# A decoder trunk on one core: down products in the seven-product form, chained sums in PSUM, weight sums on GpSimd

## The chip, the cores and the metric

The kernel runs on one core of a Trainium2 chip. TensorE (PE in the profile, PEld for its weight loads), VectorE (DVE), ScalarE (ACT), GpSimd (POOL) and SyncE (SP, which issues the loads here) run side by side, each with its own queue in order. The metric is the time of one execution on the device, in microseconds.

## The reference, cut to what matters

Two layers work on 512 tokens of 1024 features (all float32): a feed-forward half, a mixer (gated convolution and forgetting attention), cross-attention over 256 memory tokens, and a second feed-forward half; so there are four feed-forward halves. The change touches these alone:

```python
def swiglu(h, w_gu, w_down):
    gate, up = jnp.split(h @ w_gu, 2, axis=-1)        # w_gu: 1024 x 5632
    return (jax.nn.silu(gate) * up) @ w_down          # w_down: 2816 x 1024
x = x + 0.5 * swiglu(rmsnorm(x, g_ffn1[l]), w_ffn1_gu[l], w_ffn1_down[l])
```

## The kernel before, in words

**Precision.** Each operand of a product is split into two float32r parts: hi is a cast on ScalarE, lo = source - hi a subtraction on VectorE (`split`, L197; for weights L157 and L158 in `Weights.prefetch`). `mm3` (L192, its matmul is L195) makes one product as three matmuls: hi.hi, hi.lo, lo.hi.

**Layout.** x stands with its features on the partitions, as eight tiles of 128 x 512 tokens. The 2816 hidden columns are cut into six chunks (`CHUNKS`): chunk 0 has 256, the others 512 each.

**Gate and up products.** Chunk 0 is computed plainly. For each other chunk, gates and ups are the two column halves of one product; with tokens and input features halved too, seven products of quarter size (Winograd's form, numbers 1 to 7) take the place of eight. They need sums of activations (`FfnNormed.prepare`, L465, once per half) and of weight blocks (`Weights.quads`, L68): four sums (t1 to t4) for each of two row halves, on VectorE (L76). A product (`product`, L500) has two units of weights, 128 x 1024 each, and 24 matmuls that move 512 columns: weights are the moving side, activations the stationary one. It uses two PSUM banks of its own (out of eight), for two token tiles. Reads after a product: 1 and 7 are copied by ScalarE (L517); 2, 6, 5, 4 and 3 are read by VectorE, which adds earlier results: fourteen additions of 128 x 512 a chunk. SiLU is on ScalarE, the product with the ups on VectorE (L454).

**Down products.** When a chunk is done, `turn` (L563) transposes it on TensorE (16 transposes through an identity matrix, L569) and splits the rows into hi and lo. `down` (L572) then makes two output tiles at a time; weights are stationary and the 512 tokens move. VectorE adds half the result to x (L579). `ffn_plan` (L1154) writes the order out by hand: a chunk's four downs stand among the seven products of the next chunk, in the order 1, turn, 7, down, 2, down, 6, down, 5, 4, 3, down. At the end of a half the last downs hand each new tile of x at once to `after.add`, the work for the next stage's norm. In the last half, `leave` (L587) makes the last chunk's downs with tokens on the partitions.

**Weights.** All weight blocks are listed in the order of their use. `load` fills a pool of 12 buffers of 128 x 1024 (`big`), issued on SyncE as blocks are let go; `prefetch` splits a unit two units ahead of its use (`AHEAD`), into a pool of three hi and three lo buffers, and makes a block's sum just before its split.

Of the kernel before, what the change touches and what calls it, by code (L numbers as in the profile page):

```python
# [24 lines left out]
CHUNKS = (256, 512, 512, 512, 512, 512)  # L25

# [7 lines left out]
T_BUFS = 56  # L34


class Weights:
    """The weights in the order of their use: loaded ahead, split into two float32r parts."""

    def __init__(self, nc, big_pool, unit_pool):  # L40
        self.nc, self.big_pool, self.unit_pool = nc, big_pool, unit_pool
        self.raws, self.units, self.limits = [], [], []
        self.loaded = self.freed = self.split = self.taken = 0
        self.tiles, self.ready = {}, {}
        self.limit, self.slow = 0, 0
# [22 lines left out]
    def quads(self, w, c0, n):  # L68
        """The seven products' blocks for n columns of the gates and of the ups."""
        r, tmp = {}, {}  # L70

        def raw(q, h):
            r[q, h] = self.raw(w, 2 * h + (4 if q[0] == "2" else 0), 2, (c0 + (DFF if q[1] == "2" else 0), n))

        def tt(out, a, b, op):
            self.nc.vector.tensor_tensor(out=out, in0=a, in1=b, op=op)  # L76
# [8 lines left out]
        def t3(h):  # L85
            tmp[h] = self.big((P, 2, n))
# [14 lines left out]
        def product(i):  # L101
            for h in range(2):
# [69 lines left out]
def trunk(ctx, tc, a, consts, out):  # L172
# [4 lines left out]
    tpool = ctx.enter_context(tc.tile_pool(name="t", bufs=T_BUFS))  # L177
    spool = ctx.enter_context(tc.tile_pool(name="small", bufs=8))
# [13 lines left out]
    def mm3(ps, lhs, rhs, first, last):  # L192
        pairs = ((lhs[0], rhs[0]), (lhs[0], rhs[1]), (lhs[1], rhs[0]))
        for i, (x, y) in enumerate(pairs):
            mm(ps, x, y, start=first and i == 0, stop=last and i == 2)  # L195
# [60 lines left out]
    for l in range(DEPTH):  # L256
        for which in (1, 2):
# [22 lines left out]
            for op, c, i in ffn_plan():  # L280
                c0 = sum(CHUNKS[:c])
                if op == "plain":
                    W.block(gu, 2 * i, 2, (c0, 256), (DFF + c0, 256))
                elif op == "product":
                    if c not in product:
                        product[c] = W.quads(gu, c0, CHUNKS[c])
                    product[c](i)
                elif op == "down" and l == DEPTH - 1 and which == 2 and c == len(CHUNKS) - 1:
                    W.limit = 4
                    W.unit(W.raw(dn, c0 // P + 2 * (i % 2), 2, (512 * (i // 2), 512)), keep=True)  # L290
                elif op == "down":
                    W.block(dn, c0 // P, CHUNKS[c] // P, (256 * i, 256))
# [36 lines left out]
    class Scale:  # L329
        """x is held with its tokens scaled, to be of like size wherever tokens are added: times d."""  # L330
# [9 lines left out]
        def change(self, norm):  # L340
            """Every token to a root mean square of one."""
# [7 lines left out]
    def rsqrt_mean(out, v, width, eps=None):  # L349
        """out = (v / width + eps) ** -0.5"""  # L350
# [52 lines left out]
    class Normed:  # L403
        """x times a gain, in two parts; its 1/rms is applied to what comes of it."""
# [20 lines left out]
    class FfnNormed:  # L425
        """x times a gain as the left sides of the seven products: tokens and features in halves."""
# [15 lines left out]
        def column(self):  # L442
            """1/rms for the gates, and at the scale of x for the ups."""
# [14 lines left out]
        def part(self, i, k):  # L458
            """The two parts of row tile k of product i's left side."""
# [32 lines left out]
    def swiglu_half(n, after=None, early=None):  # L492
        """x += 1/2 * SwiGLU; `after` takes the new tiles of x.

        Gates and ups are the two halves of one product's columns; with halves of the tokens and of
        the features, seven products of quarters (Winograd's form) make the four results.
        """
        s, act, turned, banks = {}, {}, {}, []

        def product(c, i):  # L500
            m = CHUNKS[c]
            bank = [PS()[:, :m] for _ in range(2)]
            for h in range(2):
                w = W.take()
                for k in range(2):
                    for e in range(2):
                        mm3(
                            bank[e], [z[:, e * P : (e + 1) * P] for z in n.part(i, 2 * h + k)],
                            [z[:, k, :] for z in w], h == k == 0, h == k == 1,
# [3 lines left out]
            for e in range(2):  # L513
                ps = bank[e]
                if i in (1, 7):
                    s[i, e] = T()[:, :m]
                    nc.scalar.copy(out=s[i, e], in_=ps)  # L517
                elif i == 2:
                    act[c, e] = g = T()[:, :m]
                    nc.vector.tensor_add(out=g, in0=ps, in1=s[1, e])  # L520
                    n.silu(g, g, e)
                elif i == 6:
                    v = s[1, e]
                    nc.vector.tensor_add(out=v, in0=ps, in1=v)
                    nc.vector.tensor_add(out=s[7, e], in0=v, in1=s[7, e])
                elif i == 5:
                    s[5, e] = T()[:, :m]
                    nc.vector.tensor_add(out=s[5, e], in0=ps, in1=s[7, e])
                    nc.vector.tensor_add(out=s[1, e], in0=ps, in1=s[1, e])
                elif i == 4:  # L530
                    act[c, 2 + e] = g = s.pop((7, e))
                    nc.vector.tensor_add(out=g, in0=ps, in1=g)
                    n.silu(g, g, 2 + e)
                    n.times(g, s.pop((5, e)), 2 + e)
# [679 lines left out]
```

## Time and profile before

| | us |
|---|---|
| median of 3 runs | 2163.15 (2163.04 to 2163.84) |
| span of the profiled execution | 2162.5 |
| PE busy | 2134.3 |
| PEld busy | 1782.3 |
| DVE busy | 1631.1 |
| ACT busy | 1033.1 |
| POOL busy | 95.6 |

The profile is of one execution, whose own time is its span. An engine is busy while at least one of its instructions runs; matmuls overlap each other, so durations of single matmuls don't add up, and the distance from start to start is what one costs. The granted clock of TensorE is 0.999 of full speed in the mean. A row of a group gives its line (of a helper, where a helper issues it), its engine, the operation, written and read tiles, shapes and count.

### The profile page before, as it was taken

To read this page: it belongs to the slowest core of one execution; us is meant where nothing else is said; L and a number is where in the kernel's file an instruction comes from. 1 tells how busy PE (TensorE), PEld (TensorE's weight loads), DVE (VectorE), ACT (ScalarE), POOL (GpSimd) and SP (SyncE) were. 2 spreads that over 40 slices of the span, in tenths; PEclk is the share of its full clock that TensorE was granted. 3 is DMA by queue.
4 is the path that set the end of the run, shared out by engine and by line. 5 is a ranking of instruction groups with operands and counts; after the bars stand their busy time and mean duration, and the time that the engine had idled before them with its cause. 6 is when DMAs were issued, how large, how long until landed. Compare 5 with 4: busy or idle time off the path is not lost.

```text
span 2162.5 us, 26168 instructions
## 1 busy us (share of the span) xinstructions
PE 2134.3 (99%) x10082; PEld 1782.3 (82%) x10082; DVE 1631.1 (75%) x2249; ACT 1033.1 (48%) x1544; POOL 95.6 (4%) x107
## 2 busy tenths in 40 slices
PE   7999999999999999999999999999999999999998
PEld 6888888788888888888888888878888888888887
DVE  6987777668755688888798887767786547987785
ACT  6433434566544554444454443346664445534343
POOL 0000000023001000000000000001220010000000
PEclk9999999999999999999999999999999999999999
DMA  5333332123552133323413333402243521333321
GB/s 179 120 106 111 117 97 69 49 78 92 152 146 88 59 108 107 97 91 101 131 58 117 95 111 98 140 27 69 80 129 114 137 75 53 117 107 117 107 78 40
DMA packets 218371, 214.56 MB, mean 99 GB/s; under 512 B 9230, under 2 KB 167174, under 8 KB 218246
## 3 DMA queue, kind: packets, MB, share of 16 engines
q1 hardware_dynamic: 218214, 212.88, 32.2%
q8 instruction: 79, 1.29, 0.3%
q14 instruction: 46, 0.38, 0.1%
q10 hardware_dynamic: 32, 0.01, 0.0%
HBM read 210.77 MB, written 2.10 MB: 98 GB/s over the span
## 4 chain that ended last, share of the span: by engine, by line
PE 92%; DVE 4%; ACT 3%; issue 1%; DMA 0%; POOL 0%; SPq 0%; DVEq 0%; POOLq 0%; ACTq 0%
PE ps L195 88%; PE ps L569 2%; ACT whi L157 1%; DVE wlo L158 1%; DVE t L835 1%; ACT t L813 1%; PE ps L807 0%; PE ps L844 0%; DVE t L376 0%; PE ps L1040 0%; PE ps L828 0%; DVE t L852 0%; DMA big<-in_x 0%; ACT big L794 0%; DVE t L675 0%
## 5 line engine op out<-in xcount | busy, mean ns | idle before, releaser
L157 ACT CAST whi<-big 128x1024 fp32r<-128x1024 f32 x516 | 536.7, 1040 | 885.3 <-PE ps L195 673.4
L195 PE MATMUL ps<-t,whi 128*128 128x512 f32 x2784 | 861.7, 390 | 1.7 <-ACT whi L747 1.4
L195 PE MATMUL ps<-whi,t 128*128 128x512 f32 x2624 | 830.7, 391 | 1.8 <-ACT t L199 1.8
L158 DVE TENSOR_TENSOR wlo<-big,whi 128x1024 fp32r<-128x1024 f32 x516 | 622.5, 1209 | 193.9 <-ACT whi L157 191.8
L195 PEld LDWEIGHTS ps<-t,whi 128*128 128x128 f32 x2784 | 520.6, 188 | 109.6 <-ACT whi L747 1.9
L195 PEld LDWEIGHTS ps<-whi,t 128*128 128x128 f32 x2624 | 493.8, 188 | 105.1 <-ACT t L199 2.5
L195 PE MATMUL ps<-t,wlo 128*128 128x512 f32 x1392 | 542.2, 389 | 1.1 <-DVE wlo L748 1.1
L195 PE MATMUL ps<-wlo,t 128*128 128x512 f32 x1312 | 511.6, 390 | 0.0
L195 PEld LDWEIGHTS ps<-t,wlo 128*128 128x128 f32 x1392 | 261.2, 188 | 56.1 <-DVE wlo L748 1.9
L195 PEld LDWEIGHTS ps<-wlo,t 128*128 128x128 f32 x1312 | 247.1, 188 | 50.4
L76 DVE TENSOR_TENSOR big<-big 128x1024 f32<-128x1024 f32 x160 | 193.6, 1218 | 1.7
L579 DVE SCALAR_TENSOR_TENSOR x<-ps,x 128x512 f32<-128x512 f32 x184 | 125.1, 687 | 89.9 <-PE ps L195 89.8
L200 DVE TENSOR_TENSOR t<-ps,t 128x512 fp32r<-128x512 f32 x128 | 82.5, 683 | 24.4 <-ACT t L199 24.0
L359 POOL TENSOR_TENSOR s<-s,mhalf 128x4 f32<-128x4 f32 (+1 forms) x19 | 16.4, 864 | 1731.1 <-DVE s L356 1693.3
L199 ACT CAST t<-ps 128x512 fp32r<-128x512 f32 x128 | 70.7, 603 | 25.9 <-PE ps L195 18.6
L818 POOL TENSOR_TENSOR t<-t,s 128x128 f32<-128x128 f32 (+1 forms) x64 | 60.4, 975 | 216.7 <-DVE s L816 103.9
L517 ACT COPY t<-ps 128x512 f32<-128x512 f32 x80 | 46.0, 587 | 34.1 <-PE ps L195 31.4
L813 ACT ACTIVATE t<-t,s 128x128 f32<-128x128 f32 (+1 forms) x64 | 35.5, 555 | 26.9 <-DVE s L809 26.5
L195 PE MATMUL ps<-big,whi 128*128 128x256 f32 x256 | 47.7, 287 | 0.0
L376 DVE TENSOR_TENSOR t<-t 128x512 f32<-128x512 f32 x61 | 44.2, 725 | 1.4 <-ACT t L372 1.4
L569 PE MATMUL ps<-cst,t 128*128 128x128 f32 x352 | 42.3, 272 | 0.0
L569 PEld LDWEIGHTS ps<-cst,t 128*128 128x128 f32 x352 | 39.8, 141 | 3.0
(170 smaller groups left out, 1599.9 us busy)
## 6 DMA issues: line engine op xcount, KB each, us to landing
big<-in_w_ffn_gu SPq DMA_DIRECT2D x160, 512.0 KB, 3.5
big<-in_w_ffn_down SPq DMA_DIRECT2D x80, 512.0 KB, 3.4
big<-in_w_mix_in SPq DMA_DIRECT2D x48, 512.0 KB, 3.8
big<-in_w_xkv SPq DMA_DIRECT2D x32, 512.0 KB, 3.9
big<-in_w_ffn_gu SPq DMA_DIRECT2D x32, 256.0 KB, 3.1
big<-in_w_mix_out SPq DMA_DIRECT2D x16, 512.0 KB, 4.8
big<-in_w_xq SPq DMA_DIRECT2D x16, 512.0 KB, 4.7
big<-in_w_xo SPq DMA_DIRECT2D x16, 512.0 KB, 4.6
```

The lines of the kernel that those rows point to most:

```text
L76: self.nc.vector.tensor_tensor(out=out, in0=a, in1=b, op=op)
L157: self.nc.scalar.copy(out=hi, in_=src)
L158: self.nc.vector.tensor_tensor(out=lo, in0=src, in1=hi.bitcast(F32), op=ALU.subtract)
L195: mm(ps, x, y, start=first and i == 0, stop=last and i == 2)
L199: nc.scalar.copy(out=hi, in_=src)
L200: nc.vector.tensor_tensor(out=lo, in0=src, in1=hi.bitcast(F32), op=ALU.subtract)
L376: nc.vector.tensor_add(out=self.acc, in0=self.acc, in1=sq)
L517: nc.scalar.copy(out=s[i, e], in_=ps)
L569: nc.tensor.transpose(ps[:, t * P : (t + 1) * P], g[t][:, f * P : (f + 1) * P], ident)
L579: nc.vector.scalar_tensor_tensor(out=x[j], in0=ps, scalar=0.5, in1=x[j], op0=ALU.mult, op1=ALU.add)
L813: nc.scalar.activation(out=o, in_=o, func=AF.Exp, bias=neg, scale=-1.0, accum_out=den[:, t : t + 1])
L818: nc.gpsimd.tensor_tensor(out=w[t], in0=w[t], in1=inv[:, t : t + 1].broadcast_to([P, (t + 1) * P]), op=ALU.mult)
```

## The change

- **Down products by sevens.** Two runs of row blocks ("u" and "v": four and four, or three and three), both halves of the 1024 outputs and both halves of the tokens make seven products (`group`) in place of eight. Weights stay stationary; 256 tokens move. A half has three groups, of six, eight and eight row blocks, and no plain downs; the last half has two groups of eight, plain downs for chunk 0 and `leave` for the last chunk.
- **What a group needs.** `turn` only copies the transposed rows (ScalarE) into row tiles (a new pool of five). `ready` makes the left sides of one product: for 7 and 3 a subtraction on GpSimd, for 6 and 5 an addition and a subtraction on VectorE, then hi and lo. Weight blocks are added by the same `quads` as for the gates.
- **Products that add up share banks.** Seven products run in the order 1, 7, 6, 2, 5, 4, 3. Products 1, 6, 5, 3 add into one pair of banks, 7 and 4 into a second, 2 into a third. Sums are read from the bank in between: ScalarE copies after 1, 7 and 6; VectorE adds after 2, 5 and 4 (six additions a chunk); after 3 the bank itself is the up. In a group, VectorE adds half of the bank to a quarter of x after each product, fourteen times 128 x 512.
- **Sums of weight blocks on GpSimd**, made one unit further ahead than the split.
- **Order.** Groups stand between chunks and nothing is interleaved with them but one `turn` after their first product; `ready` for a group's products 1 and 7 stands before the last gate product, each later one a product ahead. x's tiles go to `after.add` four at a time, after products 4 and 3 of the last group.
- Buffers: `T_BUFS` 56 to 53, x in pairs of tiles, a smaller scratch for dynamic DMA.

```diff
@@ Weights.quads
         def tt(out, a, b, op):
-            self.nc.vector.tensor_tensor(out=out, in0=a, in1=b, op=op)
+            self.nc.gpsimd.tensor_tensor(out=out, in0=a, in1=b, op=op)
...
@@ Weights.prefetch
         while self.split < len(self.units) and self.split < self.taken + n:
+            while self.made < len(self.units) and self.made <= self.split + 1:
+                pre = self.units[self.made][1]
+                if pre:
+                    self.sums[self.made] = pre()
+                self.made += 1
             r, pre, after, keep = self.units[self.split]
-            src = pre() if pre else self.tiles[r]
+            src = self.sums.pop(self.split) if pre else self.tiles[r]
@@ swiglu_half.product
-            bank = [PS()[:, :m] for _ in range(2)]
+            if i in (1, 7, 2):
+                acc[CHAIN[i]] = [PS() for _ in range(2)]
+            bank = [ps[:, :m] for ps in acc[CHAIN[i]]]
...
-                if i in (1, 7):
+                if i in (1, 7, 6):
                     s[i, e] = T()[:, :m]
                     nc.scalar.copy(out=s[i, e], in_=ps)
...
                 elif i == 5:
-                    s[5, e] = T()[:, :m]
-                    nc.vector.tensor_add(out=s[5, e], in0=ps, in1=s[7, e])
-                    nc.vector.tensor_add(out=s[1, e], in0=ps, in1=s[1, e])
+                    nc.vector.tensor_add(out=s[7, e], in0=ps, in1=s[7, e])
...
                 else:
-                    v, g = s.pop((1, e)), act[c, e]
-                    nc.vector.tensor_add(out=v, in0=ps, in1=v)
-                    n.times(g, v, e)
+                    n.times(act[c, e], ps, e)
@@ swiglu_half, new
+        def ready(c, i):
+            for p, nk in pairs(c):
+                if i in (7, 5, 6, 3):
+                    u = rows[(c, "u"), p][:, :nk, :]
+                    o = T(shape=(P, 2, 256))[:, :nk, :]
+                    if i == 7:
+                        nc.gpsimd.tensor_tensor(out=o, in0=u[:, :, :256], in1=u[:, :, 256:], op=ALU.subtract)
+                    elif i == 6:
+                        v = rows[(c, "v"), p][:, :nk, :]
+                        sums[c, 5, p] = T(shape=(P, 2, 256))[:, :nk, :]
+                        nc.vector.tensor_add(out=sums[c, 5, p], in0=u[:, :, 256:], in1=v[:, :, 256:])
+                        nc.vector.tensor_sub(out=o, in0=sums[c, 5, p], in1=u[:, :, :256])
+                        sums[c, 6, p] = o
...
+                hi, lo = (T(F32R, (P, 2, 256))[:, :nk, :] for _ in range(2))
+                nc.scalar.copy(out=hi, in_=o)
+                nc.vector.tensor_tensor(out=lo, in0=o, in1=hi.bitcast(F32), op=ALU.subtract)
+                made[c, i, p] = hi, lo
+        def group(c, i, last):
+            if i in (1, 7, 2):
+                acc[CHAIN[i]] = [PS() for _ in range(2)]
+            bank = acc[CHAIN[i]]
+            for p, nk in pairs(c):
+                w, z = W.take(), made.pop((c, i, p))
+                for f in range(4):
+                    for k in range(nk):
+                        for q, (y, v) in enumerate(((0, 0), (0, 1), (1, 0))):
+                            mm(
+                                bank[f // 2][:, f % 2 * 256 : f % 2 * 256 + 256],
+                                w[y][:, k, f * P : (f + 1) * P], z[v][:, k, :],
...
+                    nc.vector.scalar_tensor_tensor(
+                        out=o, in0=bank[b].rearrange("p (f t) -> p f t", f=2), scalar=0.5, in1=o,
+                        op0=ALU.mult, op1=ALU.add,
+                    )
...
+            if last and i in (4, 3):
+                for j in range(4):
+                    after.add(j + (4 if i == 3 else 0))
@@ ffn_plan, the halves with a stage behind them
+    chunk(1, [("turn", 0, 0)])
...
+    chunk(2, [("turn", 1, 0)])
+    group(((0, 3), (3, 3)))
+    chunk(3, [("turn", 2, 0)])
+    group(both(2), 3)
+    chunk(4)
+    chunk(5, [("turn", 4, 0)])
+    group(both(4), 5)
```

## Rows read from the trace of the kernel before

**Rows 1.** First part of the page: engine, busy us (share), instructions.

```profile
span 2162.5 us, 26168 instructions
PE 2134.3 (99%) x10082; PEld 1782.3 (82%) x10082; DVE 1631.1 (75%) x2249; ACT 1033.1 (48%) x1544; POOL 95.6 (4%) x107
```

**Rows 2.** Windows: stretch, length, busy us (xcount) of PE, PEld, DVE, ACT, POOL.

```profile
...
864.00:926.00 62.00, 62.00 (x284) 51.56 (x283) 49.82 (x58) 25.54 (x30) 0.00 (x0) 1.00 0.34 105
...
```

**Rows 3.** Timeline of PE, a down product: start us, us, engine, operation.

```profile
...
1233.31 0.61 PE L195 MATMUL ps<-t,whi 128*128 128x512 f32 x2
...
1238.07 0.61 PE L195 MATMUL ps<-t,whi 128*128 128x512 f32 x2
...
```

**Rows 4.** Timeline of PE, memory keys, whose matmuls move 256 columns.

```profile
...
553.71 0.40 PE L195 MATMUL ps<-big,whi 128*128 128x256 f32 x2
...
564.51 0.40 PE L195 MATMUL ps<-big,whi 128*128 128x256 f32 x2
...
```

**Rows 5.** Timeline of DVE at the end of a chunk's products.

```profile
...
1214.27 1.22 DVE L158 TENSOR_TENSOR wlo<-big,whi 128x1024 fp32r<-128x1024 f32 x1
1215.41 1.28 DVE L537 TENSOR_TENSOR t<-ps,t 128x512 f32<-128x512 f32 x2
1216.61 1.40 DVE L454 SCALAR_TENSOR_TENSOR t<-t,s 128x512 f32<-128x512 f32 x2
...
```

**Rows 6.** Groups by line and form: busy us, mean ns, idle before.

```profile
...
L158 DVE TENSOR_TENSOR wlo<-big,whi 128x1024 fp32r<-128x1024 f32 x500 | 611.6, 1226 | 193.9 <-ACT whi L157 191.8
...
L157 ACT CAST whi<-big 128x1024 fp32r<-128x1024 f32 x500 | 526.7, 1053 | 873.6 <-PE ps L195 663.1 <-issue 151.4 <-DMA big<-in_w_ffn_gu 21.6
...
L76 DVE TENSOR_TENSOR big<-big 128x1024 f32<-128x1024 f32 x160 | 193.6, 1218 | 1.7
...
L517 ACT COPY t<-ps 128x512 f32<-128x512 f32 x80 | 46.0, 587 | 34.1 <-PE ps L195 31.4
...
L487 DVE TENSOR_TENSOR t<-t 128x256 fp32r<-128x256 f32 x64 | 24.4, 415 | 0.0
...
```

**Rows 7.** Groups by form, POOL, 434.9 to 437.9 us.

```profile
...
L818 POOL TENSOR_TENSOR t<-t,s 128x512 f32<-128x512 f32 x1 | 1.0, 1042 | 0.0
...
L818 POOL TENSOR_TENSOR t<-t,s 128x128 f32<-128x128 f32 x1 | 0.4, 400 | 1.0 <-DVE s L816 1.0
```

**Rows 8.** The same for 486.2 to 490.6 us.

```profile
...
L818 POOL TENSOR_TENSOR t<-t,s 128x384 f32<-128x384 f32 x1 | 1.9, 1862 | 0.0
...
```

**Rows 9.** Timeline of DVE in that stretch.

```profile
...
487.16 1.22 DVE L158 TENSOR_TENSOR wlo<-big,whi 128x1024 fp32r<-128x1024 f32 x1 [0.21 <-ACT whi L157]
...
```

**Rows 10.** Timeline of POOL: a row is four products, 128 to 512 columns.

```profile
...
456.82 4.54 POOL L818 TENSOR_TENSOR t<-t,s 128x128 f32<-128x128 f32 x4 [19.08 <-PE ps L844]
...
496.57 3.65 POOL L818 TENSOR_TENSOR t<-t,s 128x128 f32<-128x128 f32 x4 [6.05 <-DVE s L816]
...
```

**Rows 11.** Timeline of DVE, 498 to 502 us.

```profile
...
499.42 1.88 DVE L158 TENSOR_TENSOR wlo<-big,whi 128x1024 fp32r<-128x1024 f32 x1
...
```

**Rows 12.** Groups by form, POOL, 456 to 462 us.

```profile
...
L818 POOL TENSOR_TENSOR t<-t,s 128x512 f32<-128x512 f32 x1 | 1.0, 1036 | 0.0
...
```

**Rows 13.** Timeline of DVE, 459.5 to 461.5 us.

```profile
...
460.20 1.60 DVE L835 TENSOR_TENSOR t<-ps,t 128x512 fp32r<-128x512 f32 x3
```

**Rows 14.** Timeline of DVE, end of a half: the next norm's tiles.

```profile
...
360.16 0.74 DVE L207 SCALAR_TENSOR_TENSOR t<-x,gcol,t 128x512 fp32r<-128x512 f32 x1
360.82 1.22 DVE L158 TENSOR_TENSOR wlo<-big,whi 128x1024 fp32r<-128x1024 f32 x1
...
```

**Rows 15.** Timeline of ACT at one split.

```profile
...
1238.72 1.05 ACT L157 CAST whi<-big 128x1024 fp32r<-128x1024 f32 x1 [3.67 <-PE ps L195]
...
```

**Rows 16.** Timeline of DVE at the same split.

```profile
...
1239.81 1.23 DVE L158 TENSOR_TENSOR wlo<-big,whi 128x1024 fp32r<-128x1024 f32 x1 [0.17 <-ACT whi L157]
...
```

**Rows 17.** Timeline of PE there: first matmuls of two products.

```profile
...
1238.75 0.39 PE L195 MATMUL ps<-whi,t 128*128 128x512 f32 x1
...
1244.19 0.61 PE L195 MATMUL ps<-t,whi 128*128 128x512 f32 x2
...
```

More of the change, by code (lines that the diff above doesn't have):

```diff
@@ L25 @@
 CHUNKS = (256, 512, 512, 512, 512, 512)
+FIRST = [sum(CHUNKS[:c]) // P for c in range(len(CHUNKS))]
+ORDER = (1, 7, 6, 2, 5, 4, 3)
+CHAIN = {1: "x", 6: "x", 5: "x", 3: "x", 7: "y", 4: "y", 2: "z"}
 C_ID, C_ONE, C_MASK, C_COEF = 0, 128, 256, 768
@@ L33 @@
 AHEAD = 2
-T_BUFS = 56
+T_BUFS = 53
+ROWS_BUFS = 5
 class Weights:
@@ L279, in trunk @@
             product = {}
-            for op, c, i in ffn_plan():
-                c0 = sum(CHUNKS[:c])
+            for op, c, i in ffn_plan(l == DEPTH - 1 and which == 2):
                 if op == "plain":
+                    c0 = P * FIRST[c]
                     W.block(gu, 2 * i, 2, (c0, 256), (DFF + c0, 256))
@@ L569, in turn @@
                     nc.tensor.transpose(ps[:, t * P : (t + 1) * P], g[t][:, f * P : (f + 1) * P], ident)
-                turned[c].append(split(ps))
+                place = places.get(FIRST[c] + f)
+                if place is None:
+                    turned[c].append(split(ps))
+                    continue
+                half, pair_, e = place
+                if not e:
+                    rows[half, pair_] = rpool.tile([P, 2, 512], F32, name="r", tag="r")
+                nc.scalar.copy(out=rows[half, pair_][:, e, :], in_=ps)
@@ L628, in leave @@
                     )
-        for op, c, i in ffn_plan():
-            if after is None and c == len(CHUNKS) - 1 and op != "product":
-                if op == "turn":
-                    leave(c)
-                continue
+        for at, (op, c, i) in enumerate(plan):
             if op == "plain":
@@ L642, in swiglu_half @@
                     small()
+            elif op == "ready":
+                ready(c, i)
+            elif op == "group":
+                group(c, i, after is not None and at >= len(plan) - 2 * len(ORDER))
+            elif op == "down":
+                down(c, i)
             else:
-                down(c, i)
+                leave(c)
         n.h.clear()
@@ L1151, with ffn_plan, chunk, group @@
 MIX_STEP = [1, 3, 1, 3, 1, 3, 1, 1, 1, 0]
-def ffn_plan():
-    out, last = [("plain", 0, i) for i in range(4)], len(CHUNKS) - 1
-    for c in range(1, len(CHUNKS)):
-        d = [("down", c - 1, i) for i in range(4)]
-        p = {i: ("product", c, i) for i in range(1, 8)}
-        t = ("turn", c - 1, 0)
-        out += [p[1], t, p[7], d[0], p[2], d[1], p[6], d[2], p[5], p[4], p[3], d[3]]
-    out += [("turn", last, 0)] + [("down", last, i) for i in range(4)]
+def ffn_plan(last):
+    out = [("plain", 0, i) for i in range(4)]
+    def chunk(c, first=()):
+        out.append(("product", c, ORDER[0]))
+        out.extend(first)
+        out.extend(("product", c, i) for i in ORDER[1:])
+    def group(c, turn=None):
+        ops = [("group", c, i) for i in ORDER]
+        before = out.pop()
+        out.extend([("ready", c, 1), ("ready", c, 7), before, ops[0]])
+        if turn is not None:
+            out.append(("turn", turn, 0))
+        for j in range(1, len(ORDER)):
+            if j + 1 < len(ORDER):
+                out.append(("ready", c, ORDER[j + 1]))
+            out.append(ops[j])
+    def both(c):
+        return ((FIRST[c], 4), (FIRST[c] + 4, 4))
+    chunk(1, [("turn", 0, 0)])
+    if last:
+        chunk(2, [("turn", 1, 0)] + [("down", 0, i) for i in range(4)])
+        group(both(1), 2)
+        chunk(3)
+        chunk(4, [("turn", 3, 0)])
+        group(both(3), 4)
+        chunk(5)
+        return out + [("leave", 5, 0)]
+    chunk(2, [("turn", 1, 0)])
[5 more added lines that the diff above has]
+    group(both(4), 5)
     return out
```

93 lines of the change are left out of this document (66 added, 27 removed).

## The prediction, made before the changed kernel ran

> **What bounds the kernel now.** I read the shares of busy time first: PE is busy for 2134.3 of 2162.5 us, DVE for 75%, ACT for 48%, POOL for 4% [rows 1]. An average can hide a stage, so I took the windows next: one whole chunk of a feed-forward half (seven gate and up products and four down products) lasts 62 us, PE has no gap in it, and DVE works 49.82 us, 80% [rows 2]. So PE's column time sets the pace today and DVE has about a fifth to spare. Hence two questions: how much PE time goes, and whether DVE still keeps up where its work is dense.
>
> PE's price is a pitch, since matmuls overlap and their durations (0.39 us and more) don't add. In a down product seven triples of 512 columns start over 1238.07 - 1233.31 = 4.76 us: 0.2267 each [rows 3]. The keys of the memory move 256 columns: thirty triples in 564.51 - 553.71 = 10.80 us, 0.120 each [rows 4]. That is 0.0067 more than half.
>
> DVE's pitch, from start to start: 1.14 us for 1024 columns, 0.60 for 512 (two in 1.20) [rows 5], 0.66 for one with a scalar [rows 14]. The durations are 0.08 longer [rows 6]; starts overlap ends.
>
> **PE's gain.** A half's down products are 22 row blocks x 8 x 3 = 528 matmuls of 512 columns. Three halves lose all of them, the last half loses those of 16 blocks (chunk 0 and the last chunk stay plain): 3 x 528 + 384 = 1968, x 0.2267 = 446.1 us. A group of eight blocks has 7 x 2 x 24 = 336 matmuls of 256 columns, one of six 252. There are eight of the first kind and three of the second: 3444, x 0.120 = 413.3 us. PE gains 32.8 us. Transposes stay as they are.
>
> **DVE and POOL in the gate products.** Per chunk DVE loses eight weight sums (1.14 each, 160 in all [rows 6]) and eight of its fourteen additions. What stays is 14 x 1.14 + 6 x 0.60 + 4 x 0.66 = 22.2 us beside 168 x 0.2267 = 38.1 us of PE. The eight sums go to POOL.
>
> POOL alone takes 1.04 us for 512 columns and 0.40 for 128 [rows 7], so 1.67 ns a column and 0.19 fixed; an estimate for 1024 is 1.90, of which 1.71 go with the columns. But it is not alone. A POOL product of 384 columns, 0.83 by that line, took 1.86 [rows 8] when a weight split of DVE lay across it [rows 9]; the other way round the split took 1.88 [rows 11] instead of 1.23 [rows 6] behind POOL's products, which end at 500.22 [rows 10]. So these operations go one after the other. It is not so for a DVE operation that reads PSUM and one SBUF tile: POOL's 512 columns, last of the four that end at 461.36 [rows 10], take 1.04 [rows 12] while such additions run beside them [rows 13]. I therefore charge DVE with POOL's column time, except where it lies beside PSUM reads. In a gate chunk that is at most 22.2 + 8 x 1.71 = 35.9 of 38.1 us: no loss. If the fixed part blocked too it would be 37.4, still none; stalls in single products (two sums and two additions meet in product 2) I bound at 1 us a chunk, 20 us, and take 0, since the lead below covers them.
>
> The Trainium skill (GPSIMD Engine Reference, section Performance versus the Vector engine) says that a two-input operation costs POOL about 2.6 cycles an element, since both inputs share one read port, and gives 4497 ns for 2048 columns. By that a sum of 1024 would take some 2.2 us (an estimate from that page); the rows here say 1.67 ns a column, but for a second input that is one broadcast column. The sum further down would end near 2235 us by the page. The same skill (SBUF — State Buffer, section Who interferes with whom) calls the shared port an exclusive lock for a whole instruction: by it POOL's fixed part would block too, 0.19 x 12 x 0.8 = 1.8 us a group, some 20 us more than the sum below; the 1.86 and 1.88 us here agree with one after the other, but don't part the 0.19 from the rest.
>
> **DVE and POOL in the groups.** Here nothing else is interleaved, so DVE has to do everything for 40.3 us (336 x 0.120) of PE. For eight blocks: 14 weight splits of 1.14 = 16.0; 14 splits of the activations of 0.60 = 8.4; four activation sums, 2.4; 14 additions to x of 0.60 = 8.4: 35.2 us, 87%. POOL adds eight sums of 1024 and four of 512 columns: 8 x 1.71 + 4 x 0.85 = 17.1 us. Beside the additions from PSUM (8.4 of 40.3 us) lie 3.6 of these for free. Demand: 35.2 + 17.1 - 3.6 = 48.7 us, 8.4 too many. For six blocks, PE 30.2 us: splits 7 x 1.74 = 12.2, activation splits 7 x (0.60 + 0.42) = 7.1 (0.42 is the 256-column row [rows 6]), sums 2.0, additions 8.4: 29.7; POOL 4 x (1.71 + 0.85) + 2 x (0.85 + 0.43) = 12.8, of which 3.6 free: 38.9, 8.7 too many.
>
> What DVE may lag before PE feels it: a split's cast starts at 1238.72 [rows 15], as PE begins a unit [rows 17], and its second part ends at 1239.81 + 1.23 = 1241.04 [rows 16]; PE takes it two units on, at 1244.19 [rows 17]. The lead is 3.15 us. It is spent once per group and won back in the next chunk's spare time. Stall: 8 x (8.4 - 3.15) + 3 x (8.7 - 3.15) = 42.0 + 16.7 = 58.7 us. From both sides: if POOL's sums fell wholly into DVE's idle time, nothing; if every microsecond of POOL blocked, fixed part too, with no lead, 8 x (35.2 + 19.4 - 40.3) + 3 x (29.7 + 15.1 - 30.2) = 158 us. I take the middle because the rows nearest to it show both an operation that is blocked and one that is not.
>
> **End of a half.** x comes in two lots of four tiles, not two by two. The norm work of four tiles, 4 x (0.66 [rows 14] + 0.60) = 5.0 us, stands on DVE in front of the next stage's first two weight splits: 3.5 + 5.0 = 8.5 us of work beside a product of 5.76, less the lead: about 2 us at each of three ends, 6 us (0 to 9).
>
> **At nothing.** ACT gets 40 copies (0.59 [rows 6]) and the new casts: some 26 us in a group of 40.3, DVE's load hides it. The shared banks add waits: a product may write only when the read of its predecessor in that bank is over; there is always another product between (5.44 or 5.76 us, against two copies, 1.2 us). Behind a waiting matmul stands all of PE; if that cover failed, 1.2 us x 3 x 20 = 72 us. DMA moves the same bytes; a block's load is issued two products (10.9 us) before its sum, and waits for loads in all were 21.6 us, on ACT [rows 6]. If loads came late, POOL's queue and then ACT's would hold, 1 to 2 us a time.
>
> **Sum.** 2162.5 - 32.8 + 58.7 + 6 = 2194.4 us against the profiled execution's 2162.5, which is 0.03% under the runs' median of 2163.15; so 2195.
>
> **Rivals.** (1) POOL hides: it runs ahead in its own queue, its sums need only landed blocks and finished splits, so they fall into DVE's gaps, and the lead covers the rest. For it: DVE's 87% alone fits, and 80% cost PE nothing [rows 2]. Against it: a group's gaps are 5 us and POOL's work 17. The time: 2162.5 - 32.8 + 6, and 1 us in each of the eight groups that get rows from transposes in their midst (transposes, copy, two sums, cast, subtraction against one product of 5.76): 2144. It ends on the other side, and decides where POOL blocks DVE for less than about 3 us net of the lead per group (32.8 / 11).
> (2) POOL blocks all: full column time, with the fixed part, or a two-input sum slower than the broadcast rows. 2225 to 2290. For it: DVE's queue in a group is seldom without a two-input operation. Against: the lead, and the PSUM additions.
> (3) Both nearly cancel, or the bank waits eat the gain: within 0.2%, about the least difference from no change that a measurement of this kernel can tell.
>
> **How the numbers follow.** Forecast 0.42 (2167 to 2225), rival 1 0.35, rival 3 0.09, rival 2 0.14. So faster 0.35, same 0.09, slower 0.56. The range from 2135 to 2255 leaves out about 0.07 above and 0.08 below (nothing gained could go under 2130, PE's gain alone). The forecast's own range is 2167 to 2225.
>
> **What would show it.** Right: 256-column matmuls at a pitch of 0.120 and 3444 of them; in the groups PE idle of about 5 us each, released by DVE's weight splits or activation splits; wlo's mean well over 1.23; gate chunks at 100% PE. Wrong: PE full in the groups with POOL at work there (rival 1), splits at their old 1.23 us beside POOL (no blocking), or PE waiting for reads of the banks that products share.

## The result, and the profile after

The changed kernel takes 2326.7 us (median of four runs, 2324.23 to 2330.59) beside 2163.24 for the kernel before (2163.04 to 2163.84): a ratio of 1.0756, 95% interval 1.0741 to 1.0771. The forecast was 2195 (2135 to 2255): it had the sign, and 32 of the 163 us. The time also lies above rival 2's upper end of 2290.

The first lines of the page of the changed kernel (they answer to [rows 1]):

```profile
span 2328.8 us, 29813 instructions
PE 2168.4 (93%) x11558; PEld 1865.4 (80%) x11558; DVE 1803.1 (77%) x2089; ACT 1188.2 (51%) x1804; POOL 866.9 (37%) x399
```

No engine is full any more: PE falls from 99% to 93%, and DVE, which gave away work, is busy for 172 us longer. The groups by line and form say whose operations grew (busy us, mean ns, idle before):

```profile
L170 DVE TENSOR_TENSOR wlo<-big,whi 128x1024 fp32r<-128x1024 f32 x557 | 849.0, 1531 | 259.5 <-ACT whi L169 258.5
L83 POOL TENSOR_TENSOR big<-big 128x1024 f32<-128x1024 f32 x236 | 680.8, 2893 | 757.9 <-DVE wlo L170 694.7 <-PE ps L1218 24.8 <-ACT t L391 24.0
L169 ACT CAST whi<-big 128x1024 fp32r<-128x1024 f32 x557 | 583.7, 1051 | 699.8 <-PE ps L208 295.3 <-PE ps L649 138.4 <-POOL big L83 128.2
L661 DVE SCALAR_TENSOR_TENSOR x<-ps,x 128x512 f32<-128x512 f32 x154 | 102.2, 680 | 2.1 <-PE ps L649 1.4
L636 DVE TENSOR_TENSOR t<-t 128x512 fp32r<-128x512 f32 x76 | 79.7, 1048 | 5.5 <-ACT t L635 5.5
L619 DVE TENSOR_TENSOR t<-r 128x512 f32<-128x512 f32 x19 | 30.5, 1603 | 0.0
```

The weight splits went from 1226 ns [rows 6] to 1531; other operations of DVE that read two tiles of SBUF grew too (L636 to 1048 ns, L619 to 1603; one that nothing lies beside takes 0.68 us). The additions to x, which read PSUM and one tile, take 680 ns. ACT's casts are unchanged, 1051 ns for 1053. A sum takes POOL 2893 ns in the mean. How much of that is waiting shows at one that no DVE operation lies beside (the groups of POOL, 2012 to 2017 us):

```profile
L83 POOL TENSOR_TENSOR big<-big 128x1024 f32<-128x1024 f32 x1 | 2.4, 2378 | 22.9 <-DVE wlo L170 22.9
```

So 2.38 us, where the forecast had estimated 1.90 from the rows of another operation [rows 7]. Next, both engines side by side in a group of products, DVE first, then POOL (timelines: start us, us):

```profile
265.67 1.21 DVE L170 TENSOR_TENSOR wlo<-big,whi 128x1024 fp32r<-128x1024 f32 x1
268.48 1.97 DVE L170 TENSOR_TENSOR wlo<-big,whi 128x1024 fp32r<-128x1024 f32 x1 [1.59 <-ACT whi L169]
270.37 1.28 DVE L661 SCALAR_TENSOR_TENSOR x<-ps,x 128x512 f32<-128x512 f32 x2
271.57 2.45 DVE L170 TENSOR_TENSOR wlo<-big,whi 128x1024 fp32r<-128x1024 f32 x1
274.23 1.23 DVE L170 TENSOR_TENSOR wlo<-big,whi 128x1024 fp32r<-128x1024 f32 x1 [0.21 <-ACT whi L169]
```

```profile
266.96 2.41 POOL L83 TENSOR_TENSOR big<-big 128x1024 f32<-128x1024 f32 x1 [10.77 <-DVE wlo L170]
270.53 2.41 POOL L83 TENSOR_TENSOR big<-big 128x1024 f32<-128x1024 f32 x1 [1.16 <-DVE wlo L170]
```

The sums end at 269.37 and 272.94; the splits begun beside them end 1.08 us after each. A split alone takes 1.21 us, so it does next to nothing until the sum is over. It is so in the whole trace: of 79 splits begun beside one sum the median ends 1.08 us after it. The two additions from PSUM at 270.37 take 1.28 us together beside the second sum, as they do without one [rows 5]. [rows 8 to 13] had shown this already (there a split ended 501.30 - 500.22 = 1.08 us after POOL's products); it is dearer than I had read from them.

What that does to a group of eight row blocks (windows: stretch, length, busy us of PE, PEld, DVE, ACT, POOL, granted clock; its 352 matmuls include a chunk's 16 transposes):

```profile
986.00:1040.50 54.50, 46.21 (x353) 45.51 (x352) 49.61 (x46) 21.83 (x28) 25.38 (x11) 0.91 0.28 78
```

DVE is held for 49.61 of 54.50 us; the matmuls need 42 (below). Who waits for whom (engine, line, releaser: us, times, longest):

```profile
POOL big L83 <- DVE wlo L170: 703.9, 131, 46.9
ACT whi L169 <- POOL big L83: 137.5, 43, 5.1
ACT t L635 <- DVE t L620: 76.3, 22, 6.6
PE ps L208 <- DVE wlo L170: 47.0, 39, 4.9
PE ps L649 <- DVE wlo L170: 42.4, 21, 3.5
PE ps L649 <- ACT t L635: 34.6, 8, 4.9
```

PE's waits end with a weight split or with the left sides of a product, as forecast for the groups; but the fourth line is of the gate products, for which the forecast had charged nothing. The longest wait of a group, in four timelines (PE, DVE, ACT, POOL):

```profile
234.67 0.28 PE L649 MATMUL ps<-t,wlo 128*128 128x256 f32 x1
239.71 1.31 PE L649 MATMUL ps<-t,whi 128*128 128x256 f32 x2 [4.76 <-ACT t L635]
```

```profile
233.40 2.86 DVE L619 TENSOR_TENSOR t<-r 128x512 f32<-128x512 f32 x1
236.30 2.71 DVE L620 TENSOR_TENSOR t<-t,r 128x512 f32<-128x512 f32 x1
```

```profile
239.04 0.62 ACT L635 CAST t<-t 128x512 fp32r<-128x512 f32 x1 [6.12 <-DVE t L620]
```

```profile
226.60 11.86 POOL L83 TENSOR_TENSOR big<-big 128x1024 f32<-128x1024 f32 x4 [4.88 <-DVE wlo L170]
```

Four sums stand in a row on POOL, and beside them DVE's addition and subtraction for product 6, 0.68 us each alone, take 2.86 and 2.71. Product 6 starts 4.8 us late. The granted clock is at its lower level (1.2 GHz) there, from 237.56 to 244.38: product 6's matmuls start 0.21 us apart (241.03, 241.25, 241.46) where 0.12 is the pitch at the higher level (2.4 GHz).

And a place in the gate products, right behind a group (DVE, POOL, ACT, PE):

```profile
1053.22 4.71 DVE L170 TENSOR_TENSOR wlo<-big,whi 128x1024 fp32r<-128x1024 f32 x3 [3.37 <-ACT whi L169]
```

```profile
1043.03 11.56 POOL L83 TENSOR_TENSOR big<-big 128x1024 f32<-128x1024 f32 x4 [5.53 <-DVE wlo L170]
```

```profile
1052.14 1.05 ACT L169 CAST whi<-big 128x1024 fp32r<-128x1024 f32 x1 [4.42 <-POOL big L83]
```

```profile
1055.72 0.50 PE L208 MATMUL ps<-wlo,t 128*128 128x512 f32 x1 [1.19 <-DVE wlo L170]
```

Products 7 and 6 have four summed units in a row; POOL needs 11.56 us for them, 2.89 each, PE 2.72 a unit (12 x 0.2267). The cast waits for the sum, DVE for the cast, PE for DVE: DVE stands idle for 3.37 us and PE waits all the same. Adding up each engine's load doesn't show this.

For a table by stage I added, in each trace, the distances from one matmul's start to the next, each in the stage of the first of the two:

| us | gate and up products | groups | all else |
|---|---|---|---|
| before | 898.5 | - | 1253.4 (with the downs, 446.1 by the forecast's count) |
| after | 970.2 | 538.6 | 809.4 |
| no_sums (below) | 897.5 | 413.7 | 807.4 |
| all_dve (below) | 900.5 | 428.4 | 807.3 |

### The profile page after: what moved, and what is told of

The parts are those of the page before. It is cut to its first block, busy times and chain, and to the rows that moved or that the text cites. A ratio compares the mean times of both kernels' runs of the same rounds, so it can differ in the third digit from the quotient of the medians.

```text
span 2328.8 us, 29813 instructions
## 1 busy us (share of the span) xinstructions
PE 2168.4 (93%) x11558; PEld 1865.4 (80%) x11558; DVE 1803.1 (77%) x2089; ACT 1188.2 (51%) x1804; POOL 866.9 (37%) x399
## 3 DMA queue, kind: packets, MB, share of 16 engines
q1 hardware_dynamic: 197222, 212.88, 30.2%
## 5 line engine op out<-in xcount | busy, mean ns | idle before, releaser
L170 DVE TENSOR_TENSOR wlo<-big,whi 128x1024 fp32r<-128x1024 f32 x582 | 869.5, 1501 | 271.6 <-ACT whi L169 266.2
L83 POOL TENSOR_TENSOR big<-big 128x1024 f32<-128x1024 f32 (+1 forms) x248 | 699.3, 2828 | 767.3 <-DVE wlo L170 703.9
L649 PE MATMUL ps<-t,whi 128*128 128x256 f32 x2296 | 452.2, 298 | 36.8 <-ACT t L635 34.6
L208 PE MATMUL ps<-t,whi 128*128 128x512 f32 x1472 | 456.9, 391 | 1.5 <-ACT whi L846 1.5
L649 PEld LDWEIGHTS ps<-t,whi 128*128 128x128 f32 x2296 | 387.3, 206 | 42.1 <-ACT t L635 36.2
L649 PE MATMUL ps<-t,wlo 128*128 128x256 f32 x1148 | 343.2, 299 | 42.4 <-DVE wlo L170 42.4
L208 PEld LDWEIGHTS ps<-t,whi 128*128 128x128 f32 x1472 | 274.5, 188 | 57.3 <-ACT whi L846 2.0
L208 PE MATMUL ps<-t,wlo 128*128 128x512 f32 x736 | 287.0, 390 | 1.1 <-DVE wlo L847 1.1
L649 PEld LDWEIGHTS ps<-t,wlo 128*128 128x128 f32 x1148 | 236.4, 206 | 46.9 <-DVE wlo L170 46.8
L208 PEld LDWEIGHTS ps<-t,wlo 128*128 128x128 f32 x736 | 138.2, 188 | 30.5 <-DVE wlo L847 1.9
L378 POOL TENSOR_TENSOR s<-s,mhalf 128x4 f32<-128x4 f32 (+1 forms) x19 | 16.5, 870 | 357.9 <-DVE s L375 319.6
L636 DVE TENSOR_TENSOR t<-r,t 128x512 fp32r<-128x512 f32 x66 | 90.8, 1391 | 0.0
L636 DVE TENSOR_TENSOR t<-t 128x512 fp32r<-128x512 f32 x88 | 84.2, 962 | 5.5 <-ACT t L635 5.5
```

The source lines that it names most:

```text
L83: self.nc.gpsimd.tensor_tensor(out=out, in0=a, in1=b, op=op)
L170: self.nc.vector.tensor_tensor(out=lo, in0=src, in1=hi.bitcast(F32), op=ALU.subtract)
L208: mm(ps, x, y, start=first and i == 0, stop=last and i == 2, skip_group_check=chained)
L378: nc.gpsimd.tensor_tensor(out=out, in0=v, in1=mhalf[:, : v.shape[1]], op=ALU.pow)
L636: nc.vector.tensor_tensor(out=lo, in0=o, in1=hi.bitcast(F32), op=ALU.subtract)
L649: mm(bank[f // 2][:, f % 2 * 256 : f % 2 * 256 + 256], w[y][:, k, f * P : (f + 1) * P], z[v][:, k, :], start=i in (1, 7, 2) and p == k == ...
```

## The experiments

Two theories. **Blocking**: while POOL adds two SBUF tiles, DVE's operations on two SBUF tiles stand still, so each sum costs DVE its whole time. **Lateness**: the sums come late, and ACT and PE wait for them. Beside these: the shared banks, the seven-product form itself, and the clock. Each run's expectation stands as it was written before the run.

**1. The sums back on VectorE** (248 of them; the 44 subtractions of activations stay).

```diff
-            self.nc.gpsimd.tensor_tensor(out=out, in0=a, in1=b, op=op)
+            self.nc.vector.tensor_tensor(out=out, in0=a, in1=b, op=op)
```

> The changed kernel with its 248 weight sums on VectorE again; the 44 activation subtractions stay on GpSimd. Theory 1 (GpSimd and VectorE lock each other out of one read path): the weight splits, 1.50 us in the mean now, fall back to about 1.25; a group's VectorE work is 35 + 8 x 1.14 = 44 us against 40.3 of TensorE, so some 4 us a group stay as stalls, and so does the gap before product 6. About 2190 us (2160 to 2220). Theory 2 (the groups' form itself, its chain of activation sums and its halved matmuls, costs the time, and GpSimd only shares the work): within 1% of the changed kernel's 2326.7, since VectorE gets 280 us more to do.

2150.75 us, ratio 0.9938 [0.9923, 0.9953], below the range expected. One word of the change costs 176 us; the rest of it is a small gain (0.6%).

**2. The two subtractions of `ready` on VectorE too.**

```diff
-                        nc.gpsimd.tensor_tensor(out=o, in0=u[:, :, :256], in1=u[:, :, 256:], op=ALU.subtract)
+                        nc.vector.tensor_tensor(out=o, in0=u[:, :, :256], in1=u[:, :, 256:], op=ALU.subtract)
...
-                        nc.gpsimd.tensor_tensor(
+                        nc.vector.tensor_tensor(
```

> As sums_dve, and the activation subtractions on VectorE as well: GpSimd does nothing in the feed-forward halves. Theory 1: VectorE's work in a group is 46.7 us against 40.3, so a little over sums_dve, 2170 to 2230, with every split beside GpSimd gone to 1.22 us. Theory 2: at or over 2326.7.

2148.33 us (2147.66 to 2149.07), ratio 0.9928 [0.9911, 0.9944]: 0.7% under the kernel before, and again below the range expected. Its page:

```profile
span 2147.3 us, 29580 instructions
PE 2106.4 (98%) x11558; PEld 1827.8 (85%) x11558; DVE 1765.5 (82%) x2381; ACT 1197.2 (56%) x1804; POOL 95.8 (4%) x107
```

and two of its groups by form:

```profile
L170 DVE TENSOR_TENSOR wlo<-big,whi 128x1024 fp32r<-128x1024 f32 x557 | 681.2, 1227 | 131.0 <-ACT whi L169 129.2
L83 DVE TENSOR_TENSOR big<-big 128x1024 f32<-128x1024 f32 x236 | 285.9, 1220 | 2.5
```

The splits are back at 1227 ns. DVE makes 292 operations more than in the changed kernel and is busy for 38 us less. The group shown above, in the windows of this kernel:

```profile
914.40:957.40 43.00, 42.36 (x353) 42.15 (x352) 42.51 (x52) 21.95 (x28) 0.00 (x0) 1.00 0.33 99
```

**3. The same with each sum made just before its split.**

```diff
-            while self.made < len(self.units) and self.made <= self.split + 1:
+            while self.made < len(self.units) and self.made <= self.split:
```

> all_dve with each weight sum made just before its split instead of one unit ahead. all_dve's trace has a wait of 0.9 us at product 6 of each group of eight and 2 us in each group of six, some 13 us in all, where VectorE does a sum for a later split first. If the lead of the sums causes these, 2140 to 2145; if the chain of activation sums does, 2146 to 2150.

2150.12 us, 0.9936 [0.992, 0.9953]: where VectorE makes the sums, the unit of lead is worth nothing that these runs can tell.

**4. The kernel before, its 160 gate sums on GpSimd, one unit ahead.**

```diff
-            self.nc.vector.tensor_tensor(out=out, in0=a, in1=b, op=op)
+            self.nc.gpsimd.tensor_tensor(out=out, in0=a, in1=b, op=op)
...
+            while self.made < len(self.units) and self.made <= self.split + 1:
+                pre = self.units[self.made][1]
+                if pre:
+                    self.sums[self.made] = pre()
+                self.made += 1
...
```

> The kernel before, with one part of the change alone: the 160 weight sums of the gate products on GpSimd, made one unit further ahead; plain down products, no shared banks. Theory 1: a chunk's stage of 62 us has 38 us of VectorE work that reads SBUF twice or PSUM, plus 8 x 2.2 us in which GpSimd locks it out, 56 us in all; it fits in the mean, but splits get to 1.6 us in the mean and TensorE idles at single products, 1 to 4 us a chunk: 2170 to 2240. Theory 2: 2163, no change, since GpSimd is free and VectorE has less to do.

2193.29 us, 1.0136 [1.0121, 1.0151]. The groups of it by form:

```profile
L163 DVE TENSOR_TENSOR wlo<-big,whi 128x1024 fp32r<-128x1024 f32 x500 | 728.7, 1460 | 202.5 <-ACT whi L162 200.6
L76 POOL TENSOR_TENSOR big<-big 128x1024 f32<-128x1024 f32 x160 | 473.1, 2968 | 825.5 <-DVE wlo L163 778.0 <-PE ps L1123 25.8 <-issue 13.6
```

So the sums cost time without any group too: 30 us, where four plain downs stand between a chunk's products and DVE has slack [rows 2].

**5. The kernel before with the shared banks alone.**

```diff
+            if i in (1, 7, 2):
+                acc[CHAIN[i]] = [PS() for _ in range(2)]
+            bank = [ps[:, :m] for ps in acc[CHAIN[i]]]
...
```

> The kernel before, with one part alone: products that add up share PSUM banks, read in between (six VectorE additions a chunk in place of fourteen, 40 more ScalarE copies). Theory 1: TensorE stays the bound, nothing to gain or lose, 2163 within 0.3%. Theory 2 in the form that the reads between products hold TensorE: 1.2 us at up to three products of each of 20 chunks, up to 2235.

2164.23 us, 1.0002 [0.9993, 1.0011]: nothing. With run 4's edit on top:

> before_pool and before_chain together: weight sums on GpSimd and shared banks, down products plain and interleaved as in the kernel before. Theory 1: eight additions of VectorE fewer a chunk, those that read PSUM, while the sums still lock the splits out: between 2163 and before_pool's 2193, near 2175. If only VectorE's total load counted, 2163.

2191.45 us, 1.0127 [1.0112, 1.0142]: the eight additions a chunk that the banks save give back 2 us of 30, less than expected.

**6. Nobody needs the sums: splits read raw blocks, so the products are of other numbers.** First without the sums (one of the four is shown):

```diff
         def t3(h):
-            tmp[h] = self.big((P, parts[h][1], n))
-            return tt(tmp[h], block("22", h), block("12", h), ALU.subtract)
+            return block("22", h)
...
```

> The changed kernel without the weight sums: splits read a raw block in their place (left out: all 248 sums; the seven products are then of other numbers). GpSimd keeps the 44 activation subtractions. If the sums on GpSimd are what costs (theory 1), what is left is TensorE's time with VectorE at 35 us in a group of 40.3: 2130 to 2150, a little under all_dve's 2148.3. If the wait for sums is not it, over 2200.

2131.01 us, 0.9847 [0.9831, 0.9864]. Page and one group's window:

```profile
span 2129.2 us, 29372 instructions
PE 2100.8 (99%) x11558; PEld 1826.0 (86%) x11558; DVE 1497.6 (70%) x2089; ACT 1195.5 (56%) x1804; POOL 155.9 (7%) x151
```

```profile
906.20:949.00 42.80, 42.80 (x357) 42.66 (x356) 35.40 (x44) 22.67 (x29) 3.17 (x2) 1.00 0.34 100
```

Its span of 2129.2 is the floor that PE sets: 2162.5 - 32.8 = 2129.7 by the forecast's count. Then with all 248 sums made on GpSimd into tiles that nothing reads:

```diff
         def t3(h):
             tmp[h] = self.big((P, parts[h][1], n))
-            return tt(tmp[h], block("22", h), block("12", h), ALU.subtract)
+            tt(tmp[h], block("22", h), block("12", h), ALU.subtract)
+            return block("22", h)
...
```

> As no_sums, but GpSimd makes all 248 sums with the same inputs and sizes, into tiles that nothing reads; splits take raw blocks and wait for no sum. It parts two ways in which GpSimd can cost time. Theory 1a, VectorE is locked out while a sum runs: splits stay at 1.45 us or more in the mean and most of the 178 us between all_dve and the changed kernel come back, 2250 to 2330. Theory 1b, the chain split after sum after split is too long: near no_sums, 2140 to 2190.

2370.73 us, 1.0957 [1.094, 1.0973]:

```profile
L175 DVE TENSOR_TENSOR wlo<-big,whi 128x1024 fp32r<-128x1024 f32 x557 | 943.0, 1702 | 195.0 <-ACT whi L174 193.8
L83 POOL TENSOR_TENSOR big<-big 128x1024 f32<-128x1024 f32 x236 | 707.6, 3013 | 604.2 <-DVE wlo L175 494.9 <-DMA big<-in_w_ffn_down 43.9 <-ACT t L396 30.8
```

This parts the theories. No split reads a sum, and it is 240 us slower than without them, more than in the changed kernel (196) and above the range expected. ACT and DVE run their operations in the changed kernel's order in both runs, but for two or three of them. One wait is left that ends with POOL's sums, of ACT for a buffer, 18.0 us, by which PE loses 10.8 us near the end; beside 240 us it is small. So lateness isn't needed. POOL's sums wait for DVE's splits less often here (29 times, 498 us; 131 times, 704 us in the changed kernel), and the splits take still longer (1702 ns).

**7. Which sums.** On top of all_dve, on GpSimd: only the gates' 160, only the groups' 88, or every second one (the edit of the first).

```diff
+            e = self.nc.gpsimd if cols[0] != 0 else self.nc.vector
+            e.tensor_tensor(out=out, in0=a, in1=b, op=op)
```

> all_dve with the 160 weight sums of the gate and up products alone on GpSimd. In the trace of the changed kernel the stages of the gate products last some 63 us longer than in all_dve's. The prediction put this part at 0 (at most 20). If the stages' times are what these sums cost: 2148 + 63 = 2211 (2195 to 2230). If they only inherit the lag of the groups: under 2165.

> all_dve with the 88 weight sums of the groups alone on GpSimd. In the changed kernel the eleven groups last 8 x 11.5 + 3 x 8.4 = 117 us longer than in all_dve. If that is the price of their own sums and of the 44 subtractions, which stay on VectorE here: 2225 to 2265. If the gate products' sums push their lag into the groups: under 2200.

> all_dve with every second weight sum (those of the first row half, 124 of 248) on GpSimd. If what a sum costs is the lockout and VectorE's free time takes up the first part of it, less than half of the 178 us between all_dve and the changed kernel: 2165 to 2220. In proportion it would be 2237. If GpSimd at a moderate load were a gain, under 2148.

2243.11 us, 1.0362 [1.0345, 1.038]; 2224.91, 1.0279 [1.0263, 1.0294]; 2227.08, 1.0292 [1.0277, 1.0308]. Over all_dve they cost 94.8, 76.6 and 78.8 us: the first and the third more than expected, the second at the lower end. The first two make up 171.4 of the changed kernel's 178.4. By stage, the gates' sums cost 53.9 in the gate products and 44.0 in the groups (472.4), which I put down to the next chunk's sums being made one unit ahead, while a group still runs. Groups of eight take 44.5 to 48.6 us there, against 43.0 in all_dve; one of the longer holds two of these sums, 5.09 us on POOL (others are as long at a clock of 1.00):

```profile
955.50:1004.00 48.50, 45.01 (x353) 43.77 (x352) 48.08 (x54) 22.15 (x28) 5.09 (x2) 0.96 0.29 88
```

Every second sum costs 44% of what all cost: there is hardly a free share.

**8. The groups without the shared banks** (all_dve, gate products with banks of their own and fourteen additions, order as before).

```diff
-            if i in (1, 7, 2):
-                acc[CHAIN[i]] = [PS() for _ in range(2)]
-            bank = [ps[:, :m] for ps in acc[CHAIN[i]]]
+            bank = [PS()[:, :m] for _ in range(2)]
...
```

> all_dve without the shared banks in the gate products (fourteen VectorE additions a chunk again, two banks for each product); down products by sevens with their own chains stay. VectorE then has 36 us of work in a chunk of 38 of TensorE and 47 in a group of 40: no spare left between groups to win the lead back. Theory: TensorE stalls 3 to 6 us more at each of eleven groups, 2165 to 2215, the gain of the sevens gone. If the banks made no difference, 2148.

2202.69 us, 1.0178 [1.0163, 1.0193]: 54 us slower than all_dve, and 53 of it in the groups (481.7). What was worth nothing in run 5 pays beside the groups. That it pays because the groups use up DVE's slack fits the expectation; the additions and the order of the products were not taken apart.

**9. The clock.** The changed kernel's trace has 26 stretches, 120 us together, in which TensorE was granted 1.2 GHz. Within or right before 25 of them PE's next matmul starts 2.2 to 5.3 us after the one before; the last is at the program's end, where the kernel before has its only one, of 6.6 us. Unread matmuls of 256 columns before the products that wait (the edit of the first run):

```diff
+                if (i, p) in ((6, 0), (5, 1)):
+                    idle = PS()
+                    for _ in range(20 if i == 6 else 16):
+                        mm(idle[:, :256], fill[:, :P], fill, start=True, stop=True)
```

> The changed kernel with matmuls of 256 columns that nothing reads, 20 in front of a group's product 6 and 16 in front of the second unit of product 5, where TensorE waits 3 to 5 us: 44 x 0.12 x 18 = 48 us of TensorE time in the idle. The trace of the changed kernel shows the granted clock at half for 120 us, in 26 stretches, nearly all right behind such waits. If the clock costs time of its own (theory: up to 60 us of the 163), half of the stretches go and the time falls by 15 to 45 us, to 2280 to 2310. If TensorE only waits more for VectorE when it is quicker, 2320 to 2335.

> As fill_gaps, but the unread matmuls stand where the trace of the changed kernel has its waits and end before they do: 36 (or 20 in the two groups with a 3 us wait) in front of product 6, 22 in front of product 5 in groups of eight blocks, 14 and 20 in front of product 6 and the second unit of product 2 in groups of six: 64 us in all, each lot shorter than the wait that it stands in. If the halved clock costs time of its own, the time falls under 2326.7 by 10 to 45 us and most half-clock stretches of the groups go. If VectorE sets the pace there, the time stays within 5 us of 2326.7 although the stretches go.

> The changed kernel with unread matmuls only in front of product 6 of the eight groups of eight blocks (36, or 20 in two of them), where the trace of fill_gaps2 shows that product 6 starts as late as without them. If the half clock behind that wait costs time of its own, up to 3.4 to 6.8 us at half speed come back in eight groups: 14 to 25 us under 2326.7. If the next weight split sets the pace all the same, within 6 us of 2326.7, with the waits longer by what the clock gives back.

2354.46 us, 1.0877 [1.0861, 1.0894]; 2358.46 with fills set to the traced waits, 1.0901 [1.0885, 1.0918]; 2338.32 with fills only before product 6 of the groups of eight, 1.081 [1.0794, 1.0826]. All three are slower than the changed kernel, and outside both of the times expected for each. They don't tell what the clock costs, since the edit changed more than PE's work: behind product 6 of every group of eight, ACT's queue has another order. In the changed kernel three casts of weight splits stand between those for products 2, 5 and 4; in these runs all three stand behind them, in the last run often behind the first cast for product 3 too (fill_six, ACT, then PE):

```profile
1016.75 0.62 ACT L638 CAST t<-t 128x512 fp32r<-128x512 f32 x1 [4.51 <-POOL t L629]
1017.28 1.04 ACT L169 CAST whi<-big 128x1024 fp32r<-128x1024 f32 x1
```

```profile
1018.37 0.79 PE L659 MATMUL ps<-t,whi 128*128 128x256 f32 x2 [3.17 <-ACT whi L169]
```

The cast for product 3 waits 4.51 us for POOL's subtraction, the weight's cast stands behind it, and PE waits for that one.

The changed kernel's own trace holds a comparison, since the stretches fall differently in like groups. A group of eight, in the windows, to be set beside that from 986.00 above (54.5 us, clock 0.91):

```profile
2062.79:2115.85 53.06, 45.54 (x353) 44.84 (x352) 49.78 (x45) 21.81 (x28) 25.39 (x11) 0.94 0.27 80
```

Both have a stretch of 6.8 us at product 6. It covers more of PE's work in this group, and PE comes to product 5 0.8 us later; but in both PE goes on at 35.9 us into the group, when the split that product 5 waits for is done. So at product 6 the lower clock costs nothing. Behind that wait the group from 986.00 has another stretch, of 3.4 us, this one has none, and it is 1.5 us shorter. Likewise a group of six with 10.2 us at 1.2 GHz takes 41.06 us, one with 3.4 us 39.14. Seven groups of eight and two of six have the dearer form: an estimate from these rows is 7 x 1.5 + 2 x 1.9, some 14 us of the changed kernel's time. The price of the other stretches is open.

## Why the prediction was wrong, by its own steps

**What bounds the kernel, and PE's gain: right.** Without the sums the groups take 413.7 us, forecast 413.3, and the profiled execution 2129.2, forecast 2129.7.

**The step that failed: "DVE and POOL in the gate products ... no loss ... and take 0".** Measured: 970.2 - 897.5 = 72.7 us, and the sign named for it, gate chunks at 100% PE, did not come. Two things were wrong. POOL's time per sum was taken from products with one broadcast column [rows 7], 1.67 ns a column; the real sum of two full tiles is 2.38 us, not 1.90. A blocked split is lengthened by up to 2.2 us (a split at 1011.47 takes 3.43 in place of 1.23), so with 2.2 in place of 1.71 the forecast's own line gives 22.2 + 8 x 2.2 = 39.8 against 38.1: no longer free, 34 us in twenty chunks. And a stage's loads were compared with its length as if the order within it cost nothing. The rows right behind a group show DVE idle while a sum, a cast and a split follow one another; the 1 us a chunk at which such stalls were bounded was too little, and the lead of 3.15 us, for whose sake they were taken at 0, didn't cover them.

**DVE and POOL in the groups: mechanism right, term mis-sized.** 58.7 us forecast, 538.6 - 413.7 = 124.9 measured. With 2.2 us for 1.71, POOL's 17.1 and 12.8 us become 22.0 and 16.5, the free part 4.6, and the same working gives 52.6 - 40.3 - 3.15 = 9.2 us in a group of eight and 41.6 - 30.2 - 3.15 = 8.2 in one of six: 98 us. Both terms together then give 34 + 98 = 132 of the 199.6 us that after's span lies over that of no_sums. The other 68 stay undivided between the order of the three engines, sums of the next chunk that reach into a group (44 us in gate_pool, measured there), and the clock (some 14 us by the estimate of experiment 9).

**The price that was weighed and not taken.** An unhindered sum takes 2.38 us. The Trainium skill (GPSIMD Engine Reference, section Performance versus the Vector engine) gives some 2.2 (an estimate from its figure for 2048 columns): much nearer than the rows that I preferred to it. The sum that I worked out by it, near 2235, is still 92 us short, since it took the gate products as free too. Splits end 1.08 us after a sum's end; that agrees with the exclusive lock on the shared port of which the same skill speaks (SBUF — State Buffer, section Who interferes with whom).

**End of a half, 6 us: mostly not there.** All else takes 809.4 us, against 1253.4 - 446.1 = 807.3 before: 2 us. **At nothing: right** for ACT's copies, bank waits and loads; none is among PE's large waits, and the banks alone change nothing (ratio 1.0002).

**The rivals.** Rival 1 (POOL hides) is refuted by run 6; that its figure, 2144, is near the time with the sums on VectorE (2148) is chance. Rival 2 comes nearest, with a chance of 0.14: a two-input sum is slower than the broadcast rows. It didn't hold that POOL blocks all, since the additions from PSUM go on, and its top of 2290 was too low for the same reason as the forecast: it charged the groups alone.

**What it costs in the end.** DVE is busy for 1803.1 us in the changed kernel and 1497.6 without the sums: 305.5 us held up by sums that it doesn't make. When it makes them, the 44 subtractions of activations included, it is 1765.5 - 1497.6 = 267.9.

## What to carry to other kernels

Moving an operation on two SBUF tiles from VectorE to GpSimd didn't take it off VectorE here: it took 2.38 us on GpSimd instead of 1.22, and VectorE was held for longer than if it had done it (305.5 against 267.9 us). Before giving work to another engine, look for a row of the very operation with the very operands; a cheaper relative (here, one broadcast input) is a lower bound and not a middle. And where a stage is near full on an engine, don't put a term of it at zero without a row: take each chain of engines in order, and give the case in which all the doubtful terms go wrong together a real chance.

## What the runs showed of the hardware

- The wait goes both ways. Beside a run of DVE operations on SBUF a sum took POOL 8.01 us; it ends at 810.94, and by its 2.38 us it would have begun at about 808.6 if it had been alone, when DVE's operation of 808.27 was nearly over. DVE's reduction from PSUM at 809.41 isn't held up; the split at 810.06 is, and ends 1.09 us after the sum (POOL, then DVE, in the changed kernel):

```profile
802.93 8.01 POOL L83 TENSOR_TENSOR big<-big 128x1024 f32<-128x1024 f32 x1 [5.72 <-DVE wlo L170]
```

```profile
807.13 1.21 DVE L170 TENSOR_TENSOR wlo<-big,whi 128x1024 fp32r<-128x1024 f32 x1
808.27 0.41 DVE L500 TENSOR_TENSOR t<-t 128x256 f32<-128x256 f32 x1
809.41 0.69 DVE L404 TENSOR_REDUCE s<-ps 128x4 f32<-128x512 f32 x1 [0.72 <-PE ps L400]
810.06 1.97 DVE L170 TENSOR_TENSOR wlo<-big,whi 128x1024 fp32r<-128x1024 f32 x1
```

- A sum of two full tiles of 1024 columns takes POOL 2.38 us, the quickest of 512 columns 1.28, so 2.15 ns a column; for products with a second input of one broadcast column it was 1.67 [rows 7].
- At 1.2 GHz matmuls of 256 columns start 0.21 us apart, at 2.4 GHz 0.12. What such a stretch costs depends on what follows: at product 6 of a group of eight 6.8 us cost nothing, since PE had to wait for a split behind them; behind product 5's wait 3.4 us cost 1.5.
